# Order of loads and gates in a two-pass convolution layer: token sums, modulation rows, gate units, norm_g and W_out

## The chip, the cores and the metric

The kernel runs on one core of a Trainium2 chip. The metric is the device time in microseconds of one execution, as the median of several runs; a profile is one more execution, traced by the hardware profiler. TensorE (PE) does matmuls, VectorE (DVE), ScalarE (ACT) and GpSimd (POOL) do elementwise work, SyncE (SP) and POOL issue DMAs. TensorE's granted clock is 1.0 at 2.4 GHz and 0.5 at 1.2 GHz.

## The reference, cut to what matters

One layer of a latent-token generator, 2048 tokens of width 1024, float32: a gated short convolution, then a mixture of experts (16 experts, 256 tokens each).

```python
m_l = (silu_c @ ada_w[i] + ada_b[i])[:, None, :]
sh1, sc1, g1, sh2, sc2, g2 = jnp.split(m_l, 6, axis=-1)
hl = modulate(rms_norm(lat, norm_g[i, 0]), sh1, sc1)        # x * (1 + scale) + shift
gate_b, gate_c, v = jnp.split(hl @ w_in, 3, axis=-1)
yl = (gate_b * dwconv_centred(gate_c * v, conv_w)) @ w_out  # three taps
lat = lat + g1 * yl
hl2 = modulate(rms_norm(lat, norm_g[i, 1]), sh2, sc2)
lat = lat + g2 * expert_choice_ffn(hl2, ...)                # router, top 256 tokens of each expert, SwiGLU
```

## The kernel before, in words

Every float32 matmul is made of three fp32r matmuls (high x high, low x high, high x low), so each operand is split: ACT copies the high part and VectorE subtracts it for the low part. Weights come in pieces of 512 KB into three "raw" buffers (load_piece, load_to, by SP), and split_to turns them into "ws" buffers (8; ACT L216, VectorE L226); a raw buffer is loaded again as soon as its piece is split. Engines and queues run in the order in which the program issues, and wait by semaphores.

Tokens lie in four quarters q of 512, channels in eight tiles ct of 128, in three parts m (0 is gate_b, 1 gate_c, 2 v).

**Pass one** does hl @ w_in for q = 0 and 1. A first stage takes ct 0 and 1 of q = 0; then fourteen steps i (0 to 13) of one ct and one q each, with eight k's of nine matmuls (in_mm, L477 to L480). At the start of a step in_out evacuates the step before: ACT cs (L487), VectorE u (L490), ACT y (L494), VectorE (L495 to L508), with small POOL copies of the carried edge columns (L489, L507) and a store by POOL (L503, L505). Steps 5 to 10 also load, normalise and transpose q = 2 and 3 and store seven sums and differences of their halves (T4, B11, T1, T2, B21, T3, B22) to fscr. After step 3 constants() sets up tables with some 70 small instructions of POOL and twenty of VectorE. Buffers: "b4" has four of 128x1024, "hl" eighteen, "wide" six.

**Pass two** does q = 2 and 3 with seven block products in place of eight (84 products: 12 units of seven; a unit is two channel tiles). product() is twelve matmuls (L759 to L761) on one of the seven token sums; unit_step adds them up in PSUM banks, and ACT (L805) or VectorE (L807 to L811) evacuates them; products 3 and 5 go on in the bank of product 1. make_block builds the weight block of a product four products ahead (VectorE L743 to L748, ACT L749, VectorE L750). The token sums come back from fscr in fourteen halves of 512 KB (load_full L706 into b4, split_full: ACT L712 and VectorE L713 where the half goes to a ws buffer, L719 and L720 in two parts where it goes to hl). Halves 0 to 3 are loaded at the end of step 12, 0 to 4 split in step 13, and 5 to 13 at products 0 to 4. Units come as gate pair (0, c), (0, c+1), then (1, c), (2, c), then (1, c+1), (2, c+1); after each unit of the last two conv_start, conv_rest and conv_gate (L768 to L788) make the convolution over the next three products.

**Modulation rows.** g1, sh2, 1+sc2 and g2 (groups 2 to 5) are computed by VectorE: eight loads of 512 KB (ada_load L517, SP, into b4), eight multiply-adds (ada_add L527, L529), the bias (L511), then ada_end: TensorE sums over partitions (L536, four matmuls), VectorE adds the bias (L537), group 4 takes norm_g (loaded there, L511; L541), and the row goes to a scratch in DRAM by POOL (L543). Group 5 runs in steps 0 to 4, two rows a step, and ends at the start of step 4; groups 2, 3 and 4 run in pass two, one row at every third product.

**Pass three** multiplies by W_out, tile by tile of 128 tokens (out_mm L968 to L971, 48 matmuls). Its eight weight pieces are split over the last five products, the first tile is loaded five and split three products before the end (out_load L892, out_split L898, L899), and g1b, A2b and sh2b are read back from the scratch at the second-last product (L934, SP). In the first tile shift_logits (L1146 to L1151) multiplies sh2 by the router on TensorE.

## Time and profile before

| | us |
|---|---|
| median of 3 runs (lowest, highest) | 1905.13 (1903.23, 1907.41) |
| the profiled execution's own time | 1906.76 |
| its span, first to last instruction | 1905.0 |
| mean granted clock of TensorE | 0.981 |

Times of rows are us from the span's start. Steps 0 to 13 of pass one run from 71 to 323, pass two from 323 to 566, pass three from 576 to 790, the search for the experts' tokens and the first loads of the experts to 950, the experts to the end.

### The profile page before, as it was taken

How to read it: one execution, taken by the hardware profiler on the slowest of the kernel's cores; microseconds unless marked ns; L12 is line 12 of the kernel's file. 1: busy time of each engine (PE TensorE's matmuls, PEld its weight loads, DVE VectorE, ACT ScalarE, POOL GpSimd, SP SyncE). 2: the span in 40 equal slices, each digit the busy share in tenths (PEclk: the TensorE clock that was granted, in tenths of full speed). 3: DMA queues.
4: the chain of work that ended last, by engine and by line, in shares of the span. 5: the costliest groups of instructions: out<-in, count | busy, mean ns of one | idle time of the engine just before them, and what ended most of it. 6: DMA issues, size and time to landing. Idle time of an engine off the chain costs nothing.

```text
span 1905.0 us, 29276 instructions
## 1 busy us (share of the span) xinstructions
PE 1823.5 (96%) x11511; PEld 1617.9 (85%) x11511; DVE 1218.8 (64%) x1722; ACT 873.2 (46%) x1154; POOL 303.6 (16%) x458
## 2 busy tenths in 40 slices
PE   7998999999987999689999999999999999999998
PEld 6776887788876888479899999999999999999997
DVE  6543355778865677788667656665765666576653
ACT  4512323433333555557445544554545455455542
POOL 1121231000001222320022102101210211121002
PEclk9999999999997999889999999999999999999999
DMA  9242454453436888376697888778787878878774
GB/s 334 87 140 89 160 194 158 145 165 127 155 130 209 257 255 266 129 235 197 199 267 221 245 241 253 232 225 264 223 239 233 259 219 240 258 231 239 226 224 98
DMA packets 304635, 393.68 MB, mean 207 GB/s; under 512 B 102724, under 2 KB 173680, under 8 KB 304496
## 3 DMA queue, kind: packets, MB, share of 16 engines
q1 hardware_dynamic: 285216, 324.65, 55.0%
q0 software_dynamic: 19280, 67.16, 12.1%
q8 instruction: 90, 1.47, 0.3%
q14 instruction: 49, 0.40, 0.1%
HBM read 311.52 MB, written 57.68 MB: 194 GB/s over the span
## 4 chain that ended last, share of the span: by engine, by line
PE 85%; DVE 6%; DMA 4%; ACT 2%; issue 2%; POOL 1%; SPq 0%; POOLq 0%; ACTq 0%; DVEq 0%
PE pm L1438 11%; PE pm L1440 11%; PE pm L1442 11%; PE pm L1507 6%; PE pm L1505 6%; PE pm L1506 6%; PE pm L477 4%; PE pm L478 4%; PE pm L480 4%; PE pm L759 3%; PE pm L761 3%; PE pm L760 3%; PE pm L968 3%; PE pm L969 3%; PE pm L971 3%
## 5 line engine op out<-in xcount | busy, mean ns | idle before, releaser
L226 DVE TENSOR_TENSOR ws<-raw,ws 128x1024 fp32r<-128x1024 f32 x410 | 487.5, 1221 | 273.1 <-ACT ws L216 273.1
L216 ACT ACTIVATE ws<-raw 128x1024 fp32r<-128x1024 f32 x410 | 414.7, 1051 | 423.4 <-PE pm L1442 321.9
L1440 PE MATMUL pm<-xT,ws 128*128 128x256 f32 x2048 | 566.8, 277 | 1.9 <-DVE xT L1418 1.7
L1438 PE MATMUL pm<-xT,ws 128*128 128x256 f32 x2048 | 568.2, 277 | 0.4 <-ACT xT L1417 0.4
L1442 PE MATMUL pm<-xT,ws 128*128 128x256 f32 x2048 | 566.5, 277 | 0.0
L1440 PEld LDWEIGHTS pm<-xT,ws 128*128 128x128 f32 x2048 | 385.0, 188 | 3.9 <-DVE xT L1418 2.1
L1438 PEld LDWEIGHTS pm<-xT,ws 128*128 128x128 f32 x2048 | 384.7, 188 | 2.0 <-ACT xT L1417 0.8
L1442 PEld LDWEIGHTS pm<-xT,ws 128*128 128x128 f32 x2048 | 384.6, 188 | 0.0
L1507 PE MATMUL pm<-ws,hT 128*128 128x512 f32 x504 | 198.5, 394 | 0.0
L1535 POOL DMA_INDIRECT out_dram<-ot,idx x30 | 104.8, 3493 | 587.3 <-DVE ot L1524 583.3
L1505 PE MATMUL pm<-ws,hT 128*128 128x512 f32 x504 | 198.4, 394 | 0.0
L1506 PE MATMUL pm<-ws,hT 128*128 128x512 f32 x504 | 197.2, 391 | 0.0
L477 PE MATMUL pm<-hl,ws 128*128 128x512 f32 x384 | 154.5, 402 | 0.0
L478 PE MATMUL pm<-hl,ws 128*128 128x512 f32 x384 | 151.2, 394 | 0.0
L759 PE MATMUL pm<-tg,sb 128*128 128x512 f32 x336 | 133.3, 397 | 5.8 <-ACT cx L805 5.7
L761 PE MATMUL pm<-tg,sb 128*128 128x512 f32 x336 | 131.7, 392 | 0.0
L760 PE MATMUL pm<-tg,sb 128*128 128x512 f32 x336 | 131.5, 392 | 0.0
L968 PE MATMUL pm<-ws,hl 128*128 128x512 f32 x256 | 104.0, 406 | 9.6 <-ACT hl L898 9.6
L1507 PEld LDWEIGHTS pm<-ws,hT 128*128 128x128 f32 x504 | 94.8, 188 | 20.0
L1506 PEld LDWEIGHTS pm<-ws,hT 128*128 128x128 f32 x504 | 94.7, 188 | 19.8
L1505 PEld LDWEIGHTS pm<-ws,hT 128*128 128x128 f32 x504 | 94.8, 188 | 18.5
L480 PE MATMUL pm<-hl,ws 128*128 128x512 f32 x384 | 108.4, 391 | 0.0
(353 smaller groups left out, 2476.3 us busy)
## 6 DMA issues: line engine op xcount, KB each, us to landing
raw<-in_moe_w_down_dram SPq DMA_DIRECT2D x128, 512.0 KB, 4.7
raw<-in_moe_w_gate_dram SPq DMA_DIRECT2D x126, 512.0 KB, 5.0
raw<-in_moe_w_up_dram SPq DMA_DIRECT2D x126, 512.0 KB, 4.1
raw<-in_sc_w_in_dram SPq DMA_DIRECT2D x42, 512.0 KB, 4.6
xt<-in_x_dram SPq DMA_DIRECT2D x32, 512.0 KB, 5.8
aw<-in_ada_w_dram SPq DMA_DIRECT2D x32, 512.0 KB, 5.3
hl<-in_ada_w_dram SPq DMA_DIRECT2D x32, 256.0 KB, 6.0
hl<-vscr SPq DMA_DIRECT2D x16, 512.0 KB, 4.4
```

Source lines behind the costliest of these rows:

```text
L216: nc.scalar.activation(t[:, 0], raws[n_high], AF.Copy)
L226: (eng or nc.vector).tensor_sub(t[:, 1, ..., s], raw[..., s], t[:, 0, ..., s].bitcast(F32))
L477: nc.tensor.matmul(ps[m], wh, t[:, 0], start=(k == 0), stop=False)
L478: nc.tensor.matmul(ps[m], wl, t[:, 0], start=False, stop=False)
L759: nc.tensor.matmul(o, t[:, 0, j], r[:, 0], start=(first and j == 0), stop=False, skip_group_check=True)
L761: nc.tensor.matmul(o, t[:, 0, j], r[:, 1], start=False, stop=last, skip_group_check=True)
L1438: nc.tensor.matmul(o, w[:, 0, j, c0], xT[:, 0, k], start=(k == 0 and f % 2 == 0), stop=False, skip_group_check=True)
L1440: nc.tensor.matmul(o, w[:, 0, j, c0], xT[:, 1, k], start=False, stop=False, skip_group_check=True)
L1442: nc.tensor.matmul(o, w[:, 1, j, c0], xT[:, 0, k], start=False, stop=(k == KD - 1), skip_group_check=True)
L1505: nc.tensor.matmul(ps[s], h, w[:, 0, j], start=(k == 0), stop=False)
L1506: nc.tensor.matmul(ps[s], h, w[:, 1, j], start=False, stop=False)
L1507: nc.tensor.matmul(ps[s], l, w[:, 0, j], start=False, stop=(k == KD - 1))
```

## The change

- The fourteen halves have a new order (T3 before T2). 0 to 3 are loaded at the end of step 11, 0 to 4 split in step 12, 5 to 9 in step 13, 10 to 13 at products 0 to 3. Blocks 0 and 1 are built in step 12, 2 and 3 in step 13.
- Units come as (1, c), (2, c), then (1, c+1), (2, c+1), then the gate pair; the convolution's result waits for the gate, and the two conv_gate follow the gate unit.
- The modulation loads go to POOL's queue. One ada_step runs at every second k of steps 0 to 4 (group 5, then group 3) and at every fourth product of pass two from product 6 on (group 2, then group 4 from product 38). norm_g is loaded by POOL at the last add of group 4.
- The read-back of g1b, A2b and sh2b goes to POOL, five products before the end.
- Two of W_out's pieces are loaded into hl buffers (load_here), and depth() counts them, so that the others are loaded sooner. Piece 0 is split at the fourth-last product, 1 and 2 at the second-last, 3 at the last, 4 and 5 after it, 6 and 7 inside pass three's first tile. The first tile is split at the second-last product.

```diff
 def depth():
-    return n_raw + (2 if more else 0)
+    return n_raw + (2 if more else 0) + len(extra)
+def load_here(t):
+    nonlocal n_load
+    i = n_load
+    src, offset, ap, shape = pieces[i]
+    nc.sync.dma_start(t, dram(src, offset, ap))
+    raws[i] = t
+    extra.append(i)
+    n_load += 1
...
-    units += [((0, c), (0, c + 1)), ((1, c), (2, c)), ((1, c + 1), (2, c + 1))]
+    units += [((1, c), (2, c)), ((1, c + 1), (2, c + 1)), ((0, c), (0, c + 1))]
...
-        ada_dst[g] = b4("dst")
+        ada_dst[g] = g2b if g == 5 else b4("dst")
...
+def ada_step(g, t):
+    if t == KD + 1:
+        ada_end(g, ada_dst[g])
+    if 0 < t <= KD:
+        ada_add(g, t - 1)
+    if (g, t) == (4, KD):
+        ada_g.append(b4("gt"))
+        bcast_load(ada_g[0], norm_g, D, nc.gpsimd)
+    if t == 0:
+        ada_load(g, 0, nc.gpsimd)
+    if t + 1 < KD:
+        ada_load(g, t + 1, nc.gpsimd)
...
+halves = [(T4, 0), (T4, 1), (B11, 0), (B11, 1), (T1, 0), (T1, 1), (B21, 0), (B21, 1), (T3, 0), (T3, 1),
+          (T2, 0), (T2, 1), (B22, 0), (B22, 1)]
+in_big = [(T4, 0), (T4, 1), (B11, 0), (B11, 1), (T1, 0), (T2, 0), (T2, 1), (B22, 0)]
+def refill(s):
+    split_full(s)
+    load_full(s + 4)
...
-    gates[ct], gates[ct2] = x, y
+    at(n + 1, lambda: conv_gate(ct, x))
+    at(n + 2, lambda: conv_gate(ct2, y))
 else:
+    convs[ct] = x
     at(n + 1, lambda: conv_start(ct, x, y))
     at(n + 2, lambda: conv_rest(ct, x, y))
-    at(n + 3, lambda: conv_gate(ct, x))
...
+        if i < x_step and k % 2 == 1:
+            t = 4 * i + k // 2
+            ada_step(*((5, t) if t < KD + 2 else (3, t - KD - 2)))
-        if i == last_i - 1 and k == 7:
+        if i == last_i - 2 and k == 7:
             for s in range(4):
-                load_full(s // 2, s % 2)
+                load_full(s)
+        if i == last_i - 1:
+            if k in (1, 2, 4, 5, 7):
+                refill((1, 2, 4, 5, 7).index(k))
+            if k in (3, 6):
+                make_block((3, 6).index(k))
         if i == last_i:
-            if k in (1, 3, 5, 6):
-                make_block((1, 3, 5, 6).index(k))
...
+            if k in (1, 2, 3, 6, 7):
+                refill(5 + (1, 2, 3, 6, 7).index(k))
+            if k in (4, 5):
+                make_block(k - 2)
...
+for n in range(4):
+    at(n, lambda s=10 + n: refill(s))
...
+W_LOADS, W_SPLITS = (3, 2), {3: 0, 1: 2, 0: 3}
...
-    if n >= 5 and n % 3 == 2:
...
+    if n >= 6 and n % 4 == 2:
+        t = n // 4 - 1
+        if t < KD + 2:
+            ada_step(2, t)
+        if t >= KD:
+            ada_step(4, t - KD)
     unit_step(u, i, st)
     left = n_steps - 1 - n
-    if left < 5:
-        split_to(w_o[(1, 3, 5, 6, 7)[4 - left]])
+    if left == 5:
+        for g, name in ((2, "g1b"), (4, "A2b"), (3, "sh2b")):
+            bc[g] = b4(name)
+            nc.gpsimd.dma_start(bc[g], bass.AP(tensor=rows.tensor, ...))
     if left == 4:
         out_load(0)
+    if left in W_LOADS:
+        load_here(hl_tile([P, D], F32, "wr"))
+    if left in W_SPLITS:
+        split_to(w_o[W_SPLITS[left]])
...
+split_to(w_o[5])
...
     for k in range(KD):
+        split_to(w_o[min(k + 5, KD - 1)])
         out_mm(tb, k)
```

## Rows read from the trace of the kernel before

**Rows 1.** The page of the profile: the busy time of each engine with its share of the span (first part), the chain of work that ended last by engine (fourth part), and the two halves of a weight split of 128x1024 (fifth part: busy us, mean ns of one, idle time before them and what ended it).

```profile
PE 1823.5 (96%) x11511; PEld 1617.9 (85%) x11511; DVE 1218.8 (64%) x1722; ACT 873.2 (46%) x1154; POOL 303.6 (16%) x458
...
PE 85%; DVE 6%; DMA 4%; ACT 2%; issue 2%; POOL 1%; SPq 0%; POOLq 0%; ACTq 0%; DVEq 0%
...
L226 DVE TENSOR_TENSOR ws<-raw,ws 128x1024 fp32r<-128x1024 f32 x410 | 487.5, 1221 | 273.1 <-ACT ws L216 273.1
L216 ACT ACTIVATE ws<-raw 128x1024 fp32r<-128x1024 f32 x410 | 414.7, 1051 | 423.4 <-PE pm L1442 321.9
```

**Rows 2.** Who TensorE waited for from 60 to 800 us, the four longest: the waiting instruction, what ended the wait, then us in total, times, longest.

```profile
PE pm L968 <- ACT hl L898: 9.6, 1, 9.6
PE pt L536 <- DVE acc L529: 8.8, 1, 8.8
PE pm L759 <- ACT cx L805: 5.7, 4, 2.3
PE pt L1146 <- DMA sh2b<-rows: 5.6, 1, 5.6
```

**Rows 3.** Windows by stage: from:to, us, then busy us (and instructions) of PE, PE's weight loads, DVE, ACT and POOL, TensorE's mean granted clock, DMA share and GB/s. In order: from the end of step 3 to the first matmul of step 4, step 13, products 16 to 23 of pass two, and from pass two's end to the end of pass three's first tile.

```profile
139.00:150.70 11.70, 2.90 (x5) 1.19 (x5) 6.04 (x8) 2.27 (x3) 4.38 (x56) 0.62 0.06 24
...
306.70:323.00 16.30, 16.30 (x73) 13.51 (x72) 13.07 (x17) 8.89 (x12) 2.62 (x3) 1.00 0.36 119
...
366.00:389.00 23.00, 20.89 (x85) 16.83 (x84) 19.32 (x25) 9.67 (x16) 2.16 (x4) 0.93 0.43 138
...
566.10:602.60 36.50, 21.35 (x73) 17.40 (x73) 18.08 (x18) 7.79 (x9) 2.70 (x5) 0.67 0.64 218
```

**Rows 4.** ACT in order of time in pass one: start us, us, line, operation, out<-in, shapes, count [idle before <- what ended it]. Each is the evacuation that follows a step's last matmul: of steps 1, 2, 3 and 4.

```profile
106.39 0.60 ACT L487 ACTIVATE cs<-pm 128x512 f32<-128x512 f32 x1 [7.38 <-PE pm L480]
...
122.71 0.60 ACT L487 ACTIVATE cs<-pm 128x512 f32<-128x512 f32 x1 [13.23 <-PE pm L480]
...
139.11 0.60 ACT L487 ACTIVATE cs<-pm 128x512 f32<-128x512 f32 x1 [1.06 <-PE pm L480]
...
168.05 0.60 ACT L487 ACTIVATE cs<-pm 128x512 f32<-128x512 f32 x1 [24.06 <-PE pm L480]
```

**Rows 5.** TensorE in order of time, same columns: ada_end(5) in pass one; pass two's first matmul, its longest wait, an ada_end (L536) and the second matmul behind it, and its last matmul; then pass three's first matmul and shift_logits.

```profile
147.97 3.78 PE L536 MATMUL pt<-acc,ones_f 128*128 128x512 f32 x4 [8.80 <-DVE acc L529]
...
323.05 0.39 PE L759 MATMUL pm<-tg,sb 128*128 128x512 f32 x1
...
333.64 0.50 PE L759 MATMUL pm<-tg,sb 128*128 128x512 f32 x1 [2.27 <-ACT cx L805]
...
419.40 1.88 PE L536 MATMUL pt<-acc,ones_f 128*128 128x512 f32 x4
...
421.34 0.40 PE L760 MATMUL pm<-tg,sb 128*128 128x512 f32 x1
...
565.91 0.39 PE L761 MATMUL pm<-tg,sb 128*128 128x512 f32 x1
575.87 0.79 PE L968 MATMUL pm<-ws,hl 128*128 128x512 f32 x1 [9.57 <-ACT hl L898]
...
590.09 1.97 PE L1146 MATMUL pt<-identf,sh2b 128*128 128x128 f32 x8 [5.58 <-DMA sh2b<-rows]
591.90 3.60 PE L1150 MATMUL pl<-rt,st 128*128 128x16 f32 x16
```

**Rows 6.** DVE in order of time at the end of pass two and at the start of pass three's second tile, columns as in Rows 4.

```profile
567.93 1.23 DVE L541 SCALAR_TENSOR_TENSOR dst<-dst,gt 128x1024 f32<-128x1024 f32 x1 [7.97 <-DMA gt<-in_norm_g_dram]
...
602.63 0.69 DVE L988 TENSOR_TENSOR u<-pm,g1b 128x512 f32<-128x512 f32 x1 [5.79 <-PE pm L971]
```

**Rows 7.** DVE in order of time in steps 3 and 4, same columns: two adds, two splits, and the last instruction of the evacuation after constants().

```profile
127.12 2.59 DVE L529 SCALAR_TENSOR_TENSOR acc<-aw,s_col,acc 128x1024 f32<-128x1024 f32 x2
129.63 2.35 DVE L226 TENSOR_TENSOR ws<-raw,ws 128x1024 fp32r<-128x1024 f32 x2
...
145.25 0.15 DVE L508 COPY carry<-pm 128x1 f32<-128x1 f32 x1
```

**Rows 8.** POOL in order of time, same columns: its first instruction after constants(), the u copy of the next evacuation.

```profile
142.02 0.24 POOL L489 COPY u<-carry 128x2 f32<-128x2 f32 x1
```

**Rows 9.** DMA issues from 90 to 135 us: out<-in, queue, operation, count, KB each, median us from issue to landing.

```profile
aw<-in_ada_w_dram SPq DMA_DIRECT2D x5, 512.0 KB, 4.3
```

**Rows 10.** DMA issues of the whole execution, same columns.

```profile
hscr<-u POOLq DMA_DIRECT2D x15, 512.0 KB, 3.1
...
raw<-in_moe_w_gate_dram POOLq DMA_DIRECT2D x2, 512.0 KB, 7.8
...
sh2b<-rows SPq DMA_DIRECT2D x1, 512.0 KB, 9.3
```

**Rows 11.** Groups of instructions by line from 323 to 345 us, the splits of the token sums: line engine op, out<-in, shapes, count | busy us, mean ns of one | idle before it and what ended it.

```profile
L720 DVE TENSOR_TENSOR tg<-fu,tg 128x512 fp32r<-128x512 f32 x11 | 7.1, 687 | 3.0 <-ACT tg L719 3.0
L719 ACT ACTIVATE tg<-fu 128x512 fp32r<-128x512 f32 x12 | 6.8, 621 | 3.3 <-DMA fu<-fscr 3.2
...
L713 DVE TENSOR_TENSOR tg<-fu,tg 128x1024 fp32r<-128x1024 f32 x3 | 3.6, 1222 | 0.3 <-ACT tg L712 0.3
```

**Rows 12.** ACT in order of time at the start of pass two, columns as in Rows 4.

```profile
330.48 0.63 ACT L749 ACTIVATE sb<-raw 128x512 fp32r<-128x512 f32 x1 [3.38 <-DVE raw L747]
...
333.01 0.58 ACT L805 ACTIVATE cx<-pm 128x512 f32<-128x512 f32 x1
```

More of the change, by code (lines that the diff above doesn't have):

```diff
@@ L183, in add_piece @@
         return len(pieces) - 1
-    raws, more = {}, []
+    raws, more, extra = {}, [], []
     def depth():
-        return n_raw + (2 if more else 0)
+        return n_raw + (2 if more else 0) + len(extra)
     load_by = [nc.sync]
@@ L228, in split_low @@
             raws.pop(i)
+            if i in extra:
+                extra.remove(i)
             n_done += 1
@@ L538, in ada_end @@
             if g == 4:
-                gt = b4("gt")
-                bcast_load(gt, norm_g, D)
-                nc.vector.scalar_tensor_tensor(dst, dst, 1.0, gt, op0=ALU.add, op1=ALU.mult)
+                nc.vector.scalar_tensor_tensor(dst, dst, 1.0, ada_g.pop(), op0=ALU.add, op1=ALU.mult)
             if g < 5:
@@ L761, in product @@
                 nc.tensor.matmul(o, t[:, 0, j], r[:, 1], start=False, stop=last, skip_group_check=True)
-        gates, later = {}, {}
+        convs, later = {}, {}
         def at(n, f):
@@ L828, in block_kernel @@
                     nc.vector.tensor_copy(t, zero1.to_broadcast([P, 4]))
-            for g, k in ready:
-                ada_add(g, k, g2b)
-                if k == KD - 1:
-                    ada_end(g, g2b)
-            ready, todo = todo[:2], todo[2:]
-            for g, k in ready:
-                ada_load(g, k)
             nxt = w_chan[0, ct, 2]
@@ L910, in block_kernel @@
                 f()
-            if n >= 5 and n % 3 == 2:
-                for g in fin:
-                    ada_end(g, ada_dst[g])
-                fin = []
-                for g, k in ready:
-                    ada_add(g, k)
-                    if k == KD - 1:
-                        fin = [g]
-                ready, todo = todo[:1], todo[1:]
-                for g, k in ready:
-                    ada_load(g, k)
+            if n >= 6 and n % 4 == 2:
[4 more added lines that the diff above has]
+                    ada_step(4, t - KD)
             unit_step(u, i, st)
             left = n_steps - 1 - n
-            if left < 5:
-                split_to(w_o[(1, 3, 5, 6, 7)[4 - left]])
+            if left == 5:
+                for g, name in ((2, "g1b"), (4, "A2b"), (3, "sh2b")):
+                    bc[g] = b4(name)
+                    nc.gpsimd.dma_start(bc[g], bass.AP(tensor=rows.tensor, offset=rows.offset + (g - 2) * D, ap=[[0, P], [1, D]]))
             if left == 4:
                 out_load(0)
-            if left == 2:
+            if left in W_LOADS:
+                load_here(hl_tile([P, D], F32, "wr"))
+            if left in W_SPLITS:
+                split_to(w_o[W_SPLITS[left]])
+            if left == 1:
                 out_split(0)
-            if left == 1:
                 out_load(1)
-                for g, name in ((2, "g1b"), (4, "A2b"), (3, "sh2b")):
-                    bc[g] = b4(name)
-                    nc.sync.dma_start(bc[g], bass.AP(tensor=rows.tensor, offset=rows.offset + (g - 2) * D, ap=[[0, P], [1, D]]))
         g1b, A2b, sh2b = bc[2], bc[4], bc[3]
+        split_to(w_o[5])
         for n in sorted(later):
```

41 lines of the change are left out of this document (16 added, 25 removed).

## The prediction

> **What bounds the kernel now.** I read the page's first and fourth parts first: TensorE is busy for 96% of the span and holds 85% of the chain that ended last [rows 1]. So a change pays only where TensorE stands still or runs at its lower clock. The waits of TensorE between 60 and 800 us name four places [rows 2], and the windows put a stage to each [rows 3].
>
> First, step 4 of pass one. A step takes 16.32 us (the evacuations that open steps 2 and 3 start at 106.39 and 122.71, after 72 matmuls each), yet from the end of step 3 to the end of step 4 28.94 us pass (139.11 to 168.05) [rows 4]: 12.6 us too much. TensorE stands 8.80 us before the four matmuls of ada_end(5) [rows 5], and the stretch ran partly at 1.2 GHz (granted clock 0.62 [rows 3]).
>
> Second, the start of pass two. A matmul follows the last after 16.32 / 72 = 0.227 us, so its 1008 take 228.5 us; each of the three ada_end there costs 1.71 us (the second matmul after it comes at 421.34 in place of 419.63 [rows 5]). That makes 233.6 us, but from 323.05 to 566.14 are 243.1 us: 9.5 us lost. 5.7 us are four waits for ACT's evacuation of a PSUM bank that the next product adds to [rows 2]; the rest is the slow restart after each and 23 us at a mean clock of 0.93 [rows 3].
>
> Third, the change to pass three: its second tile starts when the first ends, at 602.63 [rows 6], 36.5 us after pass two's last matmul. The first tile is 48 matmuls (10.9 us) and shift_logits. TensorE waited 9.57 us for the copy of the tile and 5.58 us for sh2b [rows 5], and ran at 0.67 of its clock [rows 3]. Both waits go back to one: VectorE stood 7.97 us for norm_g [rows 6], which ada_end(4) loads only when it needs it; W_out's splits, its buffers and the rows' reload queued behind.
>
> **Part by part: pass one.** Unit (5, t) of the modulation work now runs at every second k of steps 0 to 2, so ada_end(5) comes in the middle of step 2. There VectorE has the evacuation (4 us), one weight split and one add behind it, and is done 7 to 8 us into the step; TensorE arrives after four k's, 8.2 us in. I take no wait, with 0 to 2 us kept for the range. The twenty loads move from SP to POOL, which shortens no path by itself: in pass one SP waited for buffers, but no TensorE wait names SP or a weight piece [rows 2].
>
> Group 3 follows in steps 2 to 4, and here I expect a new wait. Its accumulator and its destination hold two of the four b4 buffers, so each load waits on POOL until the add two units earlier is done. And constants() stands on POOL behind the last load of step 3. Before, VectorE ended step 3's two splits at 131.98, after two adds of 2.59 us [rows 7]. Without the adds and 1.71 us later for ada_end(5), it ends them at 131.1. Then: one add (1.28, half of that row), load (3, 3) with time D from issue to landing, two adds (2.6), the issue of load (3, 6) (0.6). Next is constants(), in which POOL and VectorE wait for each other: from VectorE's end of the splits (131.98) to the end of POOL's u copy (142.26 [rows 8]) it took 10.3 us. From that copy to the end of the evacuation 3.1 us (145.40 [rows 7]), one split and one add (2.5), load (3, 7) with D again, the last add (1.4). Sum: 131.1 + 21.8 + 2D = 152.9 + 2D. TensorE is through step 4 at 139.1 + 1.7 + 16.3 = 157.1 and then needs ada_end(3).
>
> No row shows an ada row loaded by POOL. Near it are: the same rows by SP in this stretch, 4.3 us [rows 9]; stores of 512 KB by POOL, 3.1, and weight loads by POOL in the busy expert stage, 7.8 [rows 10]. I take 4.7, by the nearest row plus the slower issue; the ends 3.1 and 7.8 stay for the range. Then TensorE waits 152.9 + 9.4 - 157.1 = 5.2 us (2.0 to 11.4), and I add 1.8 us for the lower clock after it, a little less than the 2.1 us left of the 12.6 after 8.8 idle and 1.7 work. The Trainium skill (DMA: Bandwidth & Descriptors, Anatomy of one DMA — SWDGE (gpsimd) path) puts a DMA issued by GpSimd at about 2.0 us plus its bytes at 436 GB/s, an estimate of 3.2 us for 512 KB; by it the wait would be 2.2 us and the whole sum 3 us lower. Pass one then pays 2 x 1.7 + 5.2 + 1.8 = 10.4 us where it paid 12.6: gain 2.2. In pass two one ada_end is gone: 1.7.
>
> **Start of pass two.** Five of the fourteen halves are split in the step before the last and five in the last one. Both steps have room: VectorE was busy 13.1 of 16.3 us in the last one [rows 3], and both the old and the new last step carry five splits; the step before gets five splits and two blocks (some 7.5 us) beside a 4 us evacuation. Five "ws" buffers are free there (eight less the three of channel 7), and "hl" comes free with q = 0's tiles. What stays in pass two is halves 10 to 13: two of T2 at products 0 and 1, two of B22 at 2 and 3. Between 323 and 345 us VectorE ran 11 + 3 of these splits, and ACT as many, with 3.2 us of waits for fu [rows 11]. Now 3 + 2 are left, about 6 us less on VectorE, the size of its arrears.
>
> The first wait, 2.27 us at 333.64 [rows 5], hangs on ACT's evacuation of product 1 at 333.01, which stands behind the block of product 5 (waits for VectorE's L747) and a tg copy and two half copies [rows 12]. One VectorE split (1.2) and 1.1 us of ACT fall away: evacuation at 330.7, done at 331.3, while TensorE wants it at 331.2. About 0.2 us stays, and I leave 0.6 for restarts. The three later waits go with the arrears; the new place of the convolution (products 7 and 8) comes when VectorE is level, and the seven later convolutions of before cost TensorE nothing [rows 2]. Gain 9.5 - 0.8 = 8.7, from 0 (nothing moves) to 9.5.
>
> **Into pass three.** norm_g is asked for four products (11 us) before its use; VectorE stood 7.97 us for it before [rows 6], so it is covered. g1b, A2b and sh2b start five products before the end, 14 us for loads of up to 9.3 us [rows 10]. W_out's pieces 0 to 3 are asked for by the fourth-last product and 5 one later, 3 and 5 into hl buffers. What is late next: let E be the end of pass two. ACT evacuates product 82 at E - 2.7 (0.6), copies two pieces (1.05 each) and the tile (the same shape) [rows 1]: E + 1.1. VectorE follows with two splits and the tile's low half, 1.22 each, to E + 2.6. So the first k ends at E + 3.0 instead of 1.4. Three more k's to E + 7.1; pieces 3 to 7 are split at E + 5.5, 6.7, 7.9, 11.5 and 12.7 (two gate products of 1.2 lie between), each ahead of its k. shift_logits took 5.4 us at the lower clock (590.09 to the end of the sixteen [rows 5]); I take 3.5 at 2.4 GHz, since ACT's two copies don't scale. The last four k's end at E + 16.1. The x tile of pass three sits in buffers that the gate units free only with their stores: I add 1.4 us for it, or for a clock that falls in shift_logits. Gain 36.5 - 17.5 = 19.0. Bounds: 10, if W_out is again late, to 22.
>
> **Sum.** 2.2 + 1.7 + 8.7 + 19.0 = 31.6 us. After pass three nothing is touched and TensorE is the bound to the end, so all of it arrives. The profiled execution took 1906.76 us (span 1905.0) and would take 1875.2; it lies 1.6 over the median, so 1905.1 - 31.6 = 1873.5, say 1874.
>
> **Rivals.**
> Group 3's adds keep up and ada_end(3) waits for nothing: 7.0 us more, 1866.5. It needs D under 2 us, or constants() overlapping the adds better than I read it; no row supports D so small. Chance 0.12.
> Only half of the change to pass three is hidden: pieces 6 and 7 are loaded when VectorE has split 1 and 2, and if they land 8 us late (as late as norm_g was [rows 6]) the first tile stalls again: gain 10, 1883. Chance 0.20.
> The start of pass two is bound by VectorE's order, not by the halves: the change does not do there what it says, 8.7 us less, 1882.5. Against it are the waits for fu and the count of splits [rows 11]. Chance 0.12.
> Slower: POOL becomes the engine that is late in pass two. On the 19 products with modulation work POOL sits at a load until VectorE's add frees the buffer, and the convolution's two edge columns and the stores queue behind it. If VectorE then waits as at 374 us, each time costs some 1.4 us idle (5.7 over four waits [rows 2]) and 1.6 at the lower clock (7% of 23 us [rows 3]), 3.0 us. From eleven such products on the gain is eaten; thirteen give 1913. It begins when a load needs more than the eight products (21.8 us) between issue and use, against 9.3 in the slowest row [rows 10]. Chance 0.03. The Trainium skill (SBUF — State Buffer, SBUF: two separate sides) names a way there: POOL cannot write its descriptors while VectorE runs in a two-port mode. No row of before shows it.
> Nothing moves: 0.01. My forecast: 0.52.
>
> **How the numbers follow.** The forecast with its bounds on D gives 1870 to 1880; with the half-hidden change and the start of pass two the upper end is 1888, with the group that keeps up the lower 1862: range 1862 to 1888. About 0.2% (4 us) is what a measurement of this kernel can tell from no change. Faster 0.95, same 0.02, slower 0.03.
>
> **What would show it.** Right: a wait of TensorE of some 5 us for acc at the end of step 4, none at step 2; step 5's first matmul near 166 instead of 168; pass two some 232 us long with no tg wait over 1 us; the second tile of pass three 17 to 18 us after pass two's last matmul; no VectorE wait for gt. Wrong: no wait at step 4 (then D or the order of constants() is misread), waits for tg or cx at products 3 to 10, or W_out waits of ACT over 3 us.

## The result and the profile after

The changed kernel takes 1879.41 us (median of 4 runs, 1878.80 to 1880.41), the kernel before 1904.72 us in the same session (4 runs, 1903.23 to 1907.41): ratio 0.9866, 95% interval 0.9849 to 0.9883, so 25.3 us faster. The forecast was 1874 with a range of 1862 to 1888. The profiled execution took 1880.41 us; its span is 1878.2 us, 26.8 us under the 1905.0 of before, where the working had 31.6. In the medians below, two executions that ran at a lower clock and took longer are left out, one of e6 (2220.09 us) and one of e7 (1907.13 us).

First the busy times from the page of the changed kernel. They answer [rows 1]: TensorE's busy share rose by one point, POOL has the added loads, and the rest is as it was.

```profile
PE 1813.7 (97%) x11511; PEld 1609.9 (86%) x11511; DVE 1218.5 (65%) x1722; ACT 872.2 (46%) x1154; POOL 320.4 (17%) x494
```

TensorE in order of time (columns as in Rows 5): ada_end(5) in step 2; the last matmuls of step 4, ada_end(3), and the first matmul of step 5; pass two's first matmul, its longest wait and its last matmul; pass three's first matmul, the two parts of shift_logits.

```profile
113.70 1.13 PE L547 MATMUL pt<-acc,ones_f 128*128 128x512 f32 x2
...
155.65 0.84 PE L491 MATMUL pm<-hl,ws 128*128 128x512 f32 x3
164.50 1.22 PE L547 MATMUL pt<-acc,ones_f 128*128 128x512 f32 x1 [8.00 <-DVE acc L540]
...
167.29 1.42 PE L488 MATMUL pm<-hl,ws 128*128 128x512 f32 x1
...
323.98 0.39 PE L794 MATMUL pm<-tg,sb 128*128 128x512 f32 x1
...
338.69 0.50 PE L794 MATMUL pm<-tg,sb 128*128 128x512 f32 x1 [0.52 <-ACT cx L841]
...
557.04 0.39 PE L796 MATMUL pm<-tg,sb 128*128 128x512 f32 x1
558.24 0.50 PE L993 MATMUL pm<-ws,hl 128*128 128x512 f32 x1 [0.81 <-ACT hl L924]
...
564.55 1.04 PE L1171 MATMUL pt<-identf,sh2b 128*128 128x128 f32 x8
565.84 1.96 PE L1175 MATMUL pl<-rt,st 128*128 128x16 f32 x16 [0.25 <-ACT st L1172]
```

VectorE when the first tile of pass three ends (answers [rows 6]), and when group 4 takes norm_g, now without a wait:

```profile
532.62 1.22 DVE L550 SCALAR_TENSOR_TENSOR dst<-dst,gt 128x1024 f32<-128x1024 f32 x1
...
574.80 0.69 DVE L1013 TENSOR_TENSOR u<-pm,g1b 128x512 f32<-128x512 f32 x1 [3.89 <-PE pm L996]
```

From these rows and [rows 5, 6] the balance can be made without a gap (the second tile is taken at its first matmul, 574.83 and before 602.66):

| stretch | before | after | gain | forecast |
|---|---|---|---|---|
| span's start to pass two's first matmul | 323.05 | 323.98 | -0.9 | +2.2 |
| pass two, first to last matmul | 242.9 | 233.1 | +9.8 | +10.4 (8.7 + 1.7) |
| last matmul to the second tile | 36.7 | 17.8 | +19.0 | +19.0 |
| second tile to the span's end | 1302.3 | 1303.4 | -1.0 | 0 |
| sum | | | 26.8 | 31.6 |

The two large terms came as forecast. Pass one lost 0.9 us where it should have gained 2.2: TensorE stands 8.0 us at ada_end(3), not 5.2. The 1.0 us of the last row lies behind pass three, where the kernels do the same: from its last matmul to the span's end are 1116.2 us before and 1117.2 after. That part takes between 1116.2 and 1120.8 us in the fourteen traces of this document, so the 1.0 us is within their scatter.

The next two views show how the 8.0 us come about. VectorE from the end of step 3 on: two adds, the evacuation of step 3 (its u, then its y), a split, the last adds.

```profile
138.66 2.61 DVE L540 SCALAR_TENSOR_TENSOR acc<-aw,s_col,acc 128x1024 f32<-128x1024 f32 x2 [5.67 <-DMA aw<-in_ada_w_dram]
...
145.49 0.68 DVE L501 TENSOR_TENSOR u<-cs,pm 128x512 f32<-128x512 f32 x1
153.37 0.75 DVE L506 SCALAR_TENSOR_TENSOR y<-u,v_col,y 128x512 f32<-128x512 f32 x1 [7.21 <-ACT y L505]
...
156.75 2.60 DVE L540 SCALAR_TENSOR_TENSOR acc<-aw,s_col,acc 128x1024 f32<-128x1024 f32 x2
163.16 1.28 DVE L540 SCALAR_TENSOR_TENSOR acc<-aw,s_col,acc 128x1024 f32<-128x1024 f32 x1 [3.81 <-DMA aw<-in_ada_w_dram]
```

POOL in the same stretch: the loads (3, 3) to (3, 6), the copy of the edge columns for that evacuation, the load (3, 7). Between 142.1 and 152.3 stand the some 70 instructions of constants(). Last, ACT's y of that evacuation.

```profile
131.97 0.53 POOL L528 DMA_DIRECT2D aw<-in_ada_w_dram  x1 [2.58 <-DVE acc L540]
133.29 0.53 POOL L528 DMA_DIRECT2D aw<-in_ada_w_dram  x1 [0.79 <-DVE acc L540]
140.24 0.53 POOL L528 DMA_DIRECT2D aw<-in_ada_w_dram  x1 [6.42 <-DVE acc L540]
141.57 0.53 POOL L528 DMA_DIRECT2D aw<-in_ada_w_dram  x1 [0.80 <-DVE ones_b L114]
...
152.31 0.25 POOL L500 COPY u<-carry 128x2 f32<-128x2 f32 x1
...
158.33 0.54 POOL L528 DMA_DIRECT2D aw<-in_ada_w_dram  x1 [0.26 <-DVE acc L540]
```

```profile
152.61 0.73 ACT L505 ACTIVATE y<-u,v_col 128x512 f32<-128x512 f32 x1 [11.89 <-POOL u L500]
```

VectorE's own share of constants() is over by 145.5, yet it stands 7.21 us for ACT's y. ACT in turn waited for POOL's u copy, which stands behind all of POOL's small instructions. That is a finer reading than the prediction's "POOL and VectorE wait for each other", and it became the question of the experiments.

### The profile page after: what moved, and what is told of

The parts are those of the page before. It is cut to its first block, busy times and chain, and to the rows that moved or that the text cites. A ratio compares the mean times of both kernels' runs of the same rounds, so it can differ in the third digit from the quotient of the medians.

```text
span 1878.2 us, 29302 instructions
## 1 busy us (share of the span) xinstructions
PE 1813.7 (97%) x11511; PEld 1609.9 (86%) x11511; DVE 1218.5 (65%) x1722; ACT 872.2 (46%) x1154; POOL 320.4 (17%) x494
## 4 chain that ended last, share of the span: by engine, by line
PE 87%; DVE 5%; DMA 3%; ACT 2%; issue 2%; POOL 1%; SPq 0%; POOLq 0%; DVEq 0%; ACTq 0%
PE pm L1464 12%; PE pm L1466 12%; PE pm L1468 12%; PE pm L1533 6%; PE pm L1531 6%; PE pm L1532 6%; PE pm L794 4%; PE pm L796 4%; PE pm L795 4%; PE pm L488 4%; PE pm L489 4%; PE pm L491 3%; PE pm L993 3%; PE pm L996 3%; PE pm L994 3%
```

## The experiments

Three questions: what makes the 8.0 us in pass one; what carried the start of pass two; and how the 19.0 us divide over norm_g, W_out, the read-back and the units' order. All runs, each against runs of the kernel before on its own chip. The medians of the kernel before in these sessions lie between 1903.84 and 1905.57 us, so a difference of one or two us between kernels of different sessions is not told apart. The last two columns are read in each trace at the places of the balance; there is one trace of each kernel.

| kernel | us, median | ratio to before, 95% | pass two | change to pass three |
|---|---|---|---|---|
| changed kernel | 1879.41 | 0.9866 (0.9849 to 0.9883) | 233.1 | 17.8 |
| e1_tables_later | 1881.45 | 0.9884 (0.9868 to 0.9901) | 233.2 | 17.8 |
| e2_rows_by_sp | 1877.13 | 0.9860 (0.9844 to 0.9877) | 233.2 | 16.2 |
| e8_third_buffer | 1876.05 | 0.9847 (0.9830 to 0.9863) | 233.3 | 16.1 |
| e7_tables_first | 1877.96 | 0.9856 (0.9836 to 0.9875) | 233.3 | 16.2 |
| e10_tables_in_step7 | 1870.29 | 0.9814 (0.9801 to 0.9828) | 233.1 | 18.2 |
| e12_shift_in_two | 1869.47 | 0.9816 (0.9803 to 0.9830) | 233.1 | 16.0 |
| e3_sums_one_step | 1886.56 | 0.9911 (0.9894 to 0.9927) | 240.1 | 16.2 |
| e5_before_norm_early | 1899.37 | 0.9972 (0.9962 to 0.9981) | 242.5 | 30.8 |
| e11_norm_in_ada_end | 1879.54 | 0.9872 (0.9856 to 0.9887) | 233.3 | 16.2 |
| e4_w_out_late | 1885.60 | 0.9905 (0.9888 to 0.9921) | 233.5 | 21.4 |
| e6_gates_first | 1886.38 | 0.9899 (0.9880 to 0.9919) | 233.3 | 24.3 |
| e9_rows_read_late | 1890.13 | 0.9916 (0.9901 to 0.9932) | 233.2 | 29.6 |

### The tables one step later

```diff
-            if i == 3:
+            if i == 4:
                 before, ones_b, tri, slot_r, step, bias, need, zero1, cnts, aux, same, quick = constants(m2)
```

> The tables (constants) are set up after step 4 in place of after step 3, so they no longer stand on POOL behind group 3's loads; nothing else is moved. Theory (the 8.0 us at ada_end(3) come from the tables behind two-buffer loads): without them the last loads of group 3 land at about 152, its last add ends near 153.5, TensorE arrives at 156.1 and doesn't wait; the 8.0 us and some 1.5 us of the lower clock after it go: 1870 us (1868 to 1874), if the tables cost nothing in step 5. Rival (POOL's own slow landing, 4.7 to 6.6 us a load, makes the chain late with or without the tables): a wait of 5 us or more stays at ada_end(3), 1876 to 1880. Rival (the tables only move the wait to step 5): ada_end(3) doesn't wait, but the step after stands 5 us or more, 1878.

1881.45 us: the second rival, that the tables only move the wait, held. TensorE passes ada_end(3) at 155.18 without a wait, and then stands 6.82 us in step 6, for tokens that step 5 should have normalised. VectorE shows the same stall as in the changed kernel, 7.21 us for ACT's y:

```profile
155.18 1.88 PE L547 MATMUL pt<-acc,ones_f 128*128 128x512 f32 x4
...
184.73 0.48 PE L412 MATMUL pt<-identf,xt 128*128 128x128 f32 x1 [6.82 <-DVE xt L405]
```

```profile
169.88 0.75 DVE L506 SCALAR_TENSOR_TENSOR y<-u,v_col,y 128x512 f32<-128x512 f32 x1 [7.21 <-ACT y L505]
```

### Group 3's rows by SP

```diff
-                ada_load(g, t + 1, nc.gpsimd)
+                ada_load(g, t + 1, nc.sync if g == 3 else nc.gpsimd)
```

(and the same for row 0)

> Only group 3's loads (rows 0 to 7) go back to SP; the tables stay after step 3, and the two free buffers stay. Theory (POOL's queue order is what costs): POOL can begin the tables while VectorE still adds, the u copy of step 3 ends near 147 in place of 152.3, load (3, 7) lands near 156, and TensorE waits 1 to 3 us at ada_end(3) in place of 8.0: 1872 to 1875. Rival (two buffers and VectorE's order set the time, whoever loads): the wait stays at 6 us or more, 1877 to 1880.

1877.13 us, in the rival's range, and by its interval not told apart from the changed kernel. The wait, 5.35 us in place of 8.0, lies between the two. POOL starts its tables earlier, since no load stands ahead of them, and VectorE's stall for y shrinks from 7.21 to 4.19 us; but the two buffers still make VectorE wait 4.49 us for row 3, and SP's load of it is not quick either: issued at 132.03, used at 137.81, 5.8 us, against 6.7 us by POOL (131.97 to 138.66).

```profile
137.81 2.61 DVE L540 SCALAR_TENSOR_TENSOR acc<-aw,s_col,acc 128x1024 f32<-128x1024 f32 x2 [4.49 <-DMA aw<-in_ada_w_dram]
151.55 0.75 DVE L506 SCALAR_TENSOR_TENSOR y<-u,v_col,y 128x512 f32<-128x512 f32 x1 [4.19 <-ACT y L505]
```

```profile
162.17 2.07 PE L547 MATMUL pt<-acc,ones_f 128*128 128x512 f32 x2 [5.35 <-DVE acc L540]
```

### A third buffer for group 3's rows

```diff
+            k_dst = 4 if g == 3 else 0
             if dst is None:
-                if k == 0:
+                if k == k_dst:
                     ada_dst[g] = g2b if g == 5 else b4("dst")
...
-            if k == 0:
+            if k == k_dst:
                 bcast_load(dst, ada_b, g * D)
```

> Group 3 takes its destination buffer only at its fifth row, so that three buffers in place of two take its first rows; POOL still loads, the tables stay after step 3. Theory (the two buffers tie each load to the add two rows before, which is half of the wait): rows 3 and 4 are loaded a row earlier, VectorE comes to the tables some 4 us sooner, the wait at ada_end(3) falls to 3 to 5 us: 1874 to 1877. Rival (only the tables' place counts): the wait stays at 7 us or more, 1878 to 1880.

1876.05 us, in the theory's range, though the interval overlaps the changed kernel's. The wait falls to 5.79 us, so the two buffers are worth some 2 us of it, half of what was expected (in five kernels that leave this place alone the wait is 7.2 to 8.0 us, so this and the 2.7 us of the run by SP are known to within 0.8). The stall for y is whole again, 7.22 us, as the tables stand where they stood:

```profile
149.99 0.75 DVE L506 SCALAR_TENSOR_TENSOR y<-u,v_col,y 128x512 f32<-128x512 f32 x1 [7.22 <-ACT y L505]
```

### The tables after step 0

```diff
-            if i == 3:
+            if i == 0:
                 before, ones_b, tri, slot_r, step, bias, need, zero1, cnts, aux, same, quick = constants(m2)
```

> The tables are set up after step 0, in place of after step 3; all else is the changed kernel. Theory (the tables behind group 3's two-buffer loads make the 8.0 us; behind group 5's loads, with three buffers and no ada_end before the middle of step 2, they cost nothing): no wait over 1 us at either ada_end, 8.0 us and some 1.5 of the lower clock go, 1869 to 1872. Rival (the wait goes with the tables to the next ada_end): a wait of 3 us or more at ada_end(5) in step 2, 1874 to 1880.

1877.96 us: my theory failed and the rival held. ada_end(3) doesn't wait any more, but ada_end(5) does, for 6.98 us, and VectorE once more stands 7.20 us for y, although group 5's rows have three buffers:

```profile
98.31 0.75 DVE L506 SCALAR_TENSOR_TENSOR y<-u,v_col,y 128x512 f32<-128x512 f32 x1 [7.20 <-ACT y L505]
```

```profile
120.08 2.93 PE L547 MATMUL pt<-acc,ones_f 128*128 128x512 f32 x3 [6.98 <-DVE acc L540]
```

So neither group 3 nor its buffers are the main cause. The stall of some 7.2 us belongs to the tables, and whatever TensorE wants from VectorE next pays for it.

### The tables in step 7, behind the evacuation

```diff
-            if i == 5:
+            if i == 7:
+                before, ones_b, tri, slot_r, step, bias, need, zero1, cnts, aux, same, quick = constants(m2)
+                nc.sync.dma_start(rt, dram(router, 0, [[E, P], [E * P, KD], [1, E]]))
...
                 for t in cnts:
                     nc.vector.tensor_copy(t, zero1.to_broadcast([P, 4]))
...
-            if i == 3:
-                before, ones_b, tri, slot_r, step, bias, need, zero1, cnts, aux, same, quick = constants(m2)
-                nc.sync.dma_start(rt, dram(router, 0, [[E, P], [E * P, KD], [1, E]]))
...
```

> The tables, their router load and the two count copies are issued in step 7, behind that step's evacuation of step 6, where no modulation row, no normalisation and no token sum is due. New theory, from the two kernels in which the tables only moved the stall (step 5: 6.8 us for xt; step 2: 7.0 us for ada_end(5)): the stall is POOL's some 60 small instructions ahead of the u copy of the next evacuation; ACT's y waits for that copy and VectorE stood 7.2 us for y; whatever TensorE wants from VectorE in the step that follows comes 7 us late. Behind the evacuation, with a whole step before the next u copy, they cost nothing: no wait over 1.2 us in pass one after step 0, 8.0 us and 1.5 to 3 of the lower clock go, 1868 to 1871. Rival (group 3's two buffers and POOL's landing times set the 8.0 us by themselves): 4 us or more stay at ada_end(3), 1874 to 1878. Second rival (the stall moves once more, to step 8's normalisation or the sums): a wait of 4 us or more in steps 8 to 11, 1876 to 1880.

1870.29 us, 9.1 us under the changed kernel and in the expected range; both rivals are out. No wait of TensorE over 1.1 us is left in pass one. POOL is through the tables when its next u copy comes at 214.16, which is when step 7's matmuls end, so that evacuation waits for nothing. VectorE still stands 5.50 us for one of POOL's tables, but TensorE, which wants no row, tile or sum from it in step 7, waits 0.21 us afterwards. So two things came together, the place behind the evacuation and a step with room; no run separates them. ada_end(3) starts at once:

```profile
157.38 1.88 PE L547 MATMUL pt<-acc,ones_f 128*128 128x512 f32 x4
```

```profile
212.91 1.54 DVE L868 CAST cnt<-zero 128x4 fp32r<-128x4 f32 x2 [5.50 <-POOL zero L166]
```

The windows of the changed kernel around that place, then those of this one (columns as in Rows 3): the busy time of TensorE and the granted clock both come back.

```profile
155.70:170.00 14.30, 6.30 (x14) 3.41 (x13) 6.88 (x7) 0.60 (x1) 3.12 (x5) 0.64 0.31 92
```

```profile
155.00:170.00 15.00, 15.00 (x64) 11.72 (x63) 6.50 (x9) 3.22 (x4) 1.65 (x4) 1.00 0.27 76
```

### The token sums as before

```diff
-                if i == last_i - 2 and k == 7:
+                if i == last_i - 1 and k == 7:
                     for s in range(4):
                         load_full(s)
-                if i == last_i - 1:
-                    if k in (1, 2, 4, 5, 7):
-                        refill((1, 2, 4, 5, 7).index(k))
-                    if k in (3, 6):
-                        make_block((3, 6).index(k))
                 if i == last_i:
-                    if k in (1, 2, 3, 6, 7):
-                        refill(5 + (1, 2, 3, 6, 7).index(k))
-                    if k in (4, 5):
-                        make_block(k - 2)
+                    if k in (1, 3, 5, 6):
+                        make_block((1, 3, 5, 6).index(k))
+                    if k in (1, 2, 4, 6, 7):
+                        refill((1, 2, 4, 6, 7).index(k))
...
-        for n in range(4):
-            at(n, lambda s=10 + n: refill(s))
+        for s in range(5, 14):
+            at((0, 0, 1, 1, 2, 2, 3, 4, 4)[s - 5], lambda s=s: refill(s))
```

(and the old order of the halves)

> The token sums are loaded and split as in the kernel before: halves 0 to 3 loaded at the end of step 12, 0 to 4 split and blocks 0 to 3 built in step 13, 5 to 13 at products 0 to 4, in the old order; the rest is the changed kernel. Theory (VectorE's and ACT's arrears at the start of pass two were those splits): 8 to 10 us come back, with waits for cx at products 3 to 6: 1888 us (1886 to 1890). Rival (the start of pass two was freed by the modulation rows that left it, or by the gate units that went to third place): 0 to 3 us, 1880 to 1883.

1886.56 us, 7.2 more than the changed kernel, and in the trace pass two is 7.0 us longer (240.1 against 233.1) with two waits of TensorE for cx of some 2 us, the first of them like the 2.27 us of [rows 5]:

```profile
333.61 0.50 PE L793 MATMUL pm<-tg,sb 128*128 128x512 f32 x1 [2.26 <-ACT cx L840]
```

The earlier halves, with the blocks built beside them, are thus 7 of the 8.7 us taken for the start of pass two. The units' new order and the smaller modulation work are still in this kernel, so they are not what freed the start of pass two.

### norm_g early, in the kernel before

```diff
                     ada_add(g, k)
+                    if (g, k) == (4, KD - 1):
+                        ada_g.append(b4("gt"))
+                        bcast_load(ada_g[0], norm_g, D)
...
-                gt = b4("gt")
-                bcast_load(gt, norm_g, D)
```

> The kernel before with one edit: norm_g is loaded (by SP) at group 4's last add, three products ahead of ada_end(4), in place of in it. Theory (VectorE's 7.97 us for norm_g was the first cause of both waits of pass three's first tile, W_out's buffers the second): VectorE no longer waits for gt, the waits for the copied tile (9.57) and for sh2b (5.58) shrink by some 8 us and take part of the low clock with them: 8 to 12 us faster than before, 1892 to 1896. Rival (W_out's three raw buffers set the first tile, whatever norm_g does): 0 to 4 us, 1900 to 1904.

1899.37 us: 4.7 us, between theory and rival, nearer to the rival. VectorE doesn't wait for norm_g any more, and the wait for the copied tile falls from 9.57 [rows 5] to 3.72 us. But a wait for sh2b stays, 5.8 us against 5.6 [rows 2]:

```profile
PE pt L1147 <- DMA sh2b<-rows: 5.8, 1, 5.8
PE pm L969 <- ACT hl L896: 3.7, 1, 3.7
```

The read-back did not stay where it was: SP issues it 7.7 us earlier, behind W_out's pieces. First the kernel before, then this one:

```profile
580.71 0.67 SPq L934 DMA_DIRECT2D sh2b<-rows  x1
```

```profile
572.99 0.54 SPq L935 DMA_DIRECT2D sh2b<-rows  x1
```

Counted from pass two's last matmul, TensorE has the tile 5.9 us and sh2b 5.8 us sooner (4.11 in place of 9.96, 18.42 in place of 24.18). So VectorE's wait for norm_g had pushed both back by some 6 us, but without it 3.7 and 5.8 us of waiting are left, which have other causes.

### norm_g late, in the changed kernel

```diff
-            if (g, t) == (4, KD):
-                ada_g.append(b4("gt"))
-                bcast_load(ada_g[0], norm_g, D, nc.gpsimd)
...
+                gt = b4("gt")
+                bcast_load(gt, norm_g, D)
```

> The changed kernel with norm_g loaded by SP inside ada_end(4), as in the kernel before; ada_end(4) stays where the change puts it, at product 74, ten products before the end. Theory (norm_g's lateness mattered before only since ada_end(4) stood four products before the end; with ten, the four blocks built ahead and the products in between take up VectorE's wait): VectorE waits 4 to 9 us for gt, TensorE 0 to 1 us in pass two, and the change to pass three stays at 17 to 18.5 us: 1879 to 1882. Rival (an early norm_g carries much of the gain wherever ada_end(4) stands): a wait of TensorE of 2 us or more after product 74, or a change to pass three of 20 us or more: 1883 to 1888.

1879.54 us, the same time. VectorE was expected to wait 4 to 9 us for gt; its wait is below 0.1 us. norm_g is asked for at 527.78 and lands 4.5 us later, while VectorE still has blocks to finish:

```profile
530.97 1.28 DVE L548 TENSOR_TENSOR dst<-pt,dst 128x512 f32<-128x512 f32 x2
532.33 1.23 DVE L552 SCALAR_TENSOR_TENSOR dst<-dst,gt 128x1024 f32<-128x1024 f32 x1
```

So at its new place, ten products before the end of pass two and not four, ada_end(4) gets norm_g in time even if it asks for it only then; the early load adds nothing. Part of it is that norm_g lands sooner there: here one weight piece was issued just ahead of it, in the kernel before three and a tile within 4.5 us. That was not tested by itself.

### W_out as before

```diff
+            if left < 5:
+                split_to(w_o[(1, 3, 5, 6, 7)[4 - left]])
...
-            if left in W_LOADS:
-                load_here(hl_tile([P, D], F32, "wr"))
-            if left in W_SPLITS:
-                split_to(w_o[W_SPLITS[left]])
+            if left == 2:
+                out_split(0)
             if left == 1:
-                out_split(0)
                 out_load(1)
...
-        split_to(w_o[5])
...
-                split_to(w_o[min(k + 5, KD - 1)])
```

> W_out as in the kernel before: no loads into hl buffers, pieces split by the old plan (0 and 1 at the fifth-last product, 2 and 3, 4 and 5, 6, 7 at the next ones), the first tile split at the third-last product; norm_g, the rows' read-back and the units' order stay as changed. Theory (norm_g was the first cause, but W_out's few raw buffers hold back the first tile too): 4 to 10 us of the 19.0 come back, 1884 to 1890. Rival (norm_g and the read-back were all of it): within 3 us of the changed kernel, 1878 to 1882.

1885.60 us, 6.2 more, as the theory had it. The first tile waits 5.05 us for its copy, which on ACT stands behind a piece that has not landed:

```profile
559.54 1.06 ACT L225 ACTIVATE ws<-raw 128x1024 fp32r<-128x1024 f32 x1 [3.91 <-DMA raw<-in_sc_w_out_dram]
560.50 1.04 ACT L924 ACTIVATE hl<-hl 128x1024 fp32r<-128x1024 f32 x1
```

```profile
561.60 0.80 PE L991 MATMUL pm<-ws,hl 128*128 128x512 f32 x1 [5.05 <-ACT hl L924]
```

In the trace the change to pass three grows by 3.6 us (17.8 to 21.4); of the 4.8 us that its span is longer, 2.1 lie behind pass three (1119.3 us against 1117.2), where the kernels do the same. So what the trace shows of W_out's price is 3.6 us.

### Gates first

```diff
-        units += [((1, c), (2, c)), ((1, c + 1), (2, c + 1)), ((0, c), (0, c + 1))]
+        units += [((0, c), (0, c + 1)), ((1, c), (2, c)), ((1, c + 1), (2, c + 1))]
...
-                    at(n + 1, lambda: conv_gate(ct, x))
-                    at(n + 2, lambda: conv_gate(ct2, y))
+                    convs[ct], convs[ct2] = x, y
                 else:
-                    convs[ct] = x
...
+                    at(n + 3, lambda: conv_gate(ct, x))
```

> The changed kernel with the units' old order: gates first, then the two units of c and v with their convolution, conv_gate three products after each. Theory (the last unit's convolution then lies on VectorE between W_out's splits and the first tile, four instructions of 0.7 to 1.3 us and their ACT copy in place of two gate products): 3 to 5 us slower than the changed kernel, in the change to pass three: 1882 to 1885. Rival (the units' order is worth nothing there, since the pieces are split ahead): 0 to 1 us, 1879 to 1881. Third (the early convolution at products 7 and 8 costs at the start of pass two, so the old order gains there): 1876 to 1878.

1886.38 us, 7.0 more; the change to pass three takes 24.3 us. The price is higher than expected, and the rows say why. It is less the convolution's work on VectorE than an ACT instruction of it: it is queued ahead of shift_logits' copies and waits 5.35 us for the convolution's first product, which VectorE reaches only behind three of W_out's splits; and TensorE waits 4.36 us for those copies. In this stretch TensorE's clock also falls further (0.79 on average, 0.90 in the changed kernel), and TensorE is busy 2.4 us longer.

```profile
566.61 1.15 ACT L810 ACTIVATE cx<-cy,v_col 128x1025 f32<-128x1025 f32 x1 [5.35 <-DVE cy L806]
...
569.56 1.06 ACT L1170 ACTIVATE st<-pt 128x512 f32<-128x512 f32 x2
```

```profile
570.18 3.59 PE L1173 MATMUL pl<-rt,st 128*128 128x16 f32 x16 [4.36 <-ACT st L1170]
```

### The rows read back late

```diff
-            if left == 5:
-                for g, name in ((2, "g1b"), (4, "A2b"), (3, "sh2b")):
-                    bc[g] = b4(name)
-                    nc.gpsimd.dma_start(bc[g], bass.AP(tensor=rows.tensor, offset=rows.offset + (g - 2) * D, ap=[[0, P], [1, D]]))
...
                 out_load(1)
+                for g, name in ((2, "g1b"), (4, "A2b"), (3, "sh2b")):
+                    bc[g] = b4(name)
+                    nc.sync.dma_start(bc[g], bass.AP(tensor=rows.tensor, offset=rows.offset + (g - 2) * D, ap=[[0, P], [1, D]]))
```

> The changed kernel with the read-back of g1b, A2b and sh2b as in the kernel before: by SP, at the second-last product, behind the second tile's load. Theory (with norm_g and W_out early, the read-back of sh2b is what comes last for shift_logits: with norm_g alone early it was still waited for 5.8 us): a wait for sh2b of 1 to 5 us, 1880 to 1885. Rival (the early read-back is worth nothing once VectorE is not late): 1878 to 1880, no wait for sh2b.

1890.13 us, 10.7 more. The theory's direction held, its size did not: TensorE waits 8.64 us for sh2b, where 1 to 5 were expected. SP issues it at 560.59 as the sixth load of 512 KB within 4 us, and it takes 12 us to be used. In the changed kernel POOL issues it at 536.76 and it lands 7.3 us later, 20 us ahead of its use. TensorE was ready for it at 564.0 (572.64 less the wait). Landing in 7.3 us here too it would have come at 567.9, so by an estimate from these two traces some 4 us of the wait come of asking late and some 5 of the slower load; place and queue were changed together and are not separated. The clock adds to the price: TensorE is busy 3.4 us longer in the stretch than in the changed kernel.

```profile
556.87 1.46 SPq L200 DMA_DIRECT2D raw<-in_sc_w_out_dram  x2
558.38 0.53 SPq L918 DMA_DIRECT2D hl<-vscr  x1
559.14 0.70 SPq L957 DMA_DIRECT2D g1b<-rows  x1
559.93 0.48 SPq L957 DMA_DIRECT2D A2b<-rows  x1
560.59 0.54 SPq L957 DMA_DIRECT2D sh2b<-rows  x1
```

```profile
572.64 1.97 PE L1170 MATMUL pt<-identf,sh2b 128*128 128x128 f32 x8 [8.64 <-DMA sh2b<-rows]
```

### shift_logits in two

```diff
                 elif k == 3:
-                    shift_logits()
+                    shift_turn()
                 elif k == 5:
                     out_split(1)
+                elif k == 6:
+                    shift_logits()
```

(on top of the tables in step 7)

> The kernel with the tables in step 7, and shift_logits in two parts: the transposes of sh2 behind the fourth k of pass three's first tile as now, the eight matmuls by the router behind the seventh, so that TensorE does not wait for ACT's copies (0.6 us) and runs fewer short instructions in a row. Theory (the 17.5 us of the change to pass three hold some 1.5 us of lower clock and waits at shift_logits): 0.5 to 2 us faster than with the tables in step 7 alone, 1868 to 1870. Rival (the clock falls there all the same): within 0.5 us.

1869.47 us against 1870.29, with intervals that cover each other (0.9803 to 0.9830, 0.9801 to 0.9828): not told apart. It is the fastest kernel measured, 9.9 us under the changed one, nearly all of it by the tables' place.

## Why the prediction was right, and where its terms were off

**Pass one** is the mis-sized term: -0.9 us, not +2.2. The chain was foreseen, a wait for acc at the end of step 4 and none in step 2 (113.70, no wait shown). The working was 152.9 + 2D with D = 4.7 us for a row's load. The two loads of the chain took 6.7 us (issued 131.97, used 138.66) and 4.8 us (158.33 to 163.16), 2.1 us more than 2 x 4.7; with TensorE 0.6 us earlier (157.1 in the sum, 155.65 + 0.84 in the row) that makes the 8.0 us out of 5.2. The fixed terms held: the chain ended at 164.44, which without the two loads leaves 152.9. The bounds of 3.1 and 7.8 us held. (In the traces of e4, e6 and e11, which leave this place alone, the wait is 7.2 us.) The Trainium skill (DMA: Bandwidth & Descriptors, Anatomy of one DMA — SWDGE (gpsimd) path), by whose figures the estimate was 3.2 us a load and a wait of 2.2, came out too low; the measurement decides. The queue isn't the whole of it, since SP's load in the same place took 5.8 us. The Trainium skill (the same page, Issuing engines are not separate DMA queues) fits that: DMAs that the scalar, sync or gpsimd engine starts run on the same 16 DMA engines. The profile's row for all loads of modulation rows, median us from issue to landing in the last column:

```profile
aw<-in_ada_w_dram POOLq DMA_DIRECT2D x32, 512.0 KB, 4.3
```

What the working had wrong is the nature of its largest fixed term, the 10.3 us for constants(). It was read as VectorE and POOL waiting for each other; they do so only a little (VectorE 0.87 us, POOL 1.90), and VectorE is through its part by 145.5. The rest is one dependency, POOL's small instructions ahead of the u copy of the evacuation that follows: VectorE stands 7.20 to 7.23 us in each changed kernel in which POOL issues the row loads ahead of them and the tables stand after step 0, 3 or 4. Where SP issues them, POOL starts the tables sooner (129.67 in e2 and 128.39 in the kernel before, in place of 142.10), and VectorE stands 4.19 and 2.64 us. Moved to step 7, behind its evacuation, the tables cost TensorE nothing. Of the 8.0 us the tables' place is enough to explain all; loads by SP take away up to 2.7 (e2) and a third buffer up to 2.2 (e8): the parts overlap, and do not add up.

**The rival that group 3 keeps up** was given 1866.5 for a kernel without the wait; the kernels that have none took 1870.3 and 1869.5. The rival didn't occur: ada_end(3) waited, and the two loads of its chain took 6.7 and 4.8 us, where it needed D under 2.

**Start of pass two**: 9.8 us together with the removed ada_end, forecast 10.4. One wait for cx is left, of 0.52 us, where 0.2 and 0.6 for restarts were left over. The rival that VectorE's order and not the halves binds there is out (e3).

**Into pass three**: 17.8 us from the last matmul to the second tile, 17.5 from its end, as forecast to the tenth. That is not luck in the parts: the fourth k ended 7.3 us behind pass two (7.1 in the working), shift_logits took 3.1 (3.5) and the last four k's 7.2 (5.5, and 1.4 for the x tile or the clock). The sum was right, and one step of its argument wrong: "Both waits go back to one: VectorE stood 7.97 us for norm_g". With norm_g alone early both came some 6 us sooner, but waits of 3.7 and 5.8 us were left (e5); with norm_g late again, at ada_end(4)'s earlier place, nothing was lost (e11). Each of the others alone, put back, costs much of the gain: the read-back 11.8 us of the stretch, the units' order 6.5, W_out 3.6, part of each at the lower clock. The working had treated the read-back as a follower that a 14 us lead covers. The lead does cover it, but it is a cause of its own, the largest. The 1.4 us put down for the x tile or the clock were the clock, which does not fall there in every trace: the same stretch takes 16.1 to 16.2 us in the five traces of kernels with this part as changed in which the clock stays up (e2, e3, e7, e8, e11), with the same waits to within 0.1 us. First the changed kernel, then the one with norm_g late:

```profile
556.80:574.80 18.00, 16.52 (x75) 13.01 (x74) 14.08 (x15) 8.39 (x10) 2.30 (x3) 0.91 0.79 255
```

```profile
556.50:573.00 16.50, 14.99 (x76) 11.95 (x76) 14.20 (x16) 8.41 (x10) 2.30 (x3) 1.00 0.80 249
```

**The slower rival**, POOL late in pass two, did not show: POOL waited for VectorE's adds, 108 us over twelve loads between 340 and 556 us, but no wait of TensorE or VectorE there names POOL or a modulation row.

**Left open**: why load (3, 3) took 6.7 us and (3, 7) 4.8 (other loads in flight are a possible cause, not shown); whether the tables would also cost nothing in step 7 ahead of an evacuation, or behind one in an earlier step; and the clock's fall in the change to pass three in some traces only. With one trace of each kernel, that can be a matter of the execution: e10's traced one, where it fell, took 1876.54 us, the longest of its five.

## What to carry to other kernels

Small setup work on a slow engine goes where nothing soon needs that engine: here some 70 instructions of 0.1 to 1.0 us, moved behind an evacuation's copy and into a step with room, were worth 9 us of a 1879 us kernel, and a third buffer or loads by another queue took at most 3 us off the wait. When a stall seems to have one first cause, undo that cause alone: the sum of this change was right while its main cause was misnamed, because each of three others costs 6 to 11 us when it alone is put back. A read-back is asked for well ahead of its use: five products ahead it took 7.3 us to land and cost nothing; as the last of six loads, close to its use, it took 12 us and cost 8.6.

## What the runs showed of the hardware

- The same kind of 512 KB load took very different times: norm_g landed 4.5 us after its issue with one weight piece just ahead of it (e11), while in the kernel before, right behind three weight pieces and a tile, VectorE stood 8.0 us for it [rows 6]; sh2b landed in 7.3 us as the last of three by POOL (changed kernel) and was used 12 us after its issue as the last of six by SP (e9). What else was in flight differs in these pairs, and so do place and queue, so the cause is not shown.
- TensorE's clock fell to its lower level (1.2 GHz) after the 8.0 us wait (mean 0.64 from 155.7 to 170) and not at all in the same stretch without it (1.00 in e10). In the change to pass three it fell in the traces of the changed kernel, e1 and e10 (0.90 to 0.91 on average), and not in those of e2, e3, e7, e8 and e11 (1.00), though TensorE's waits there were the same to 0.4 us; where it falls the change takes 1.6 to 2.1 us more.
